# Two recurrence units abreast in the second half, and the whole short convolution beside the first recurrence

## The chip, the cores and the metric

The kernel runs on one core of one Trainium2 chip. The metric is the device time of one execution in microseconds (us). Three runs of the kernel before took 3340.84, 3342.81 and 3344.05 us, so the median is 3342.81 us.

## The reference, cut to what matters

The reference is one inference step of a two-layer trunk for a prompt of 1024 tokens and a group of 8 x 8 sample tokens that share all weights. All is float32. Only layer 0 is touched here:

```python
def mix_even(h, sc_buf, shift_prev, wkv0, p):
    z = h @ p['w_in']
    ya, sc_new = short_conv_mixer(z[..., :3 * SC_DIM], sc_buf, p['sc_conv_w'])     # B * conv3(C * h)
    yb, shift_new, wkv_new = rwkv7_mixer(z[..., 3 * SC_DIM:], shift_prev, wkv0, p)
    out = jnp.concatenate([ya, yb], axis=-1) @ p['w_out']
...
    # inside rwkv7_mixer, per head, with a 64 x 64 state S
    def step(S, inp):
        r_t, w_t, k_t, v_t, kk_t, a_t = inp
        S = (S * w_t[:, :, None, :]
             - jnp.einsum('bhij,bhj->bhi', S, kk_t)[..., None] * (kk_t * a_t)[:, :, None, :]
             + v_t[..., None] * k_t[:, :, None, :])
        return S, jnp.einsum('bhij,bhj->bhi', S, r_t)
```

After `mix_even` come a residual sum, an RMS norm (`nf0`), a SwiGLU feed-forward block with 22 x 128 hidden columns, another residual sum, and the norm of layer 1 (`nm1`).

## The kernel before

**Halves and dense tiles.** The tokens are cut into two halves. H0 has 576 columns (64 sample tokens and 512 of the prompt), H1 has the other 512 of the prompt. Each dense product is made in tiles of 128 output rows (`gemm_tile`, L209). Each float32 operand is split into a high and a low part, and each of the 8 steps of the inner dimension takes three matmuls (L204, L205, L206). A tile of H0 is 48 matmuls, 24 of 320 columns and 24 of 256; a tile of H1 is 24 matmuls of 512 columns. The activation of a half is held in 8 high and 8 low tiles, `hh0`/`hl0` for H0 and `hh1`/`hl1` for H1 (L186).

**The recurrence.** It is done in chunks of 64 tokens with many small matmuls. A `Unit` (L502) is one pair of heads for 256 tokens, so a half has 8 units, and H0 has a ninth one for the samples. A unit has three parts, all generators that yield after each dependent step: `prepare` (L521, 6 yields), `core` (L590, 28 yields for a prompt unit, 22 for the sample unit) and `finish` (L800, 4 yields). `recurrence` (L424) puts units into rounds: two to a round in H0 (`two`), one in H1. In a round all its cores step in turn, and beside them, one yield at a time, the `finish` of the round before and the `prepare` of the next (`together`, L446). A round of prompt units has 29 steps. The cores of a round depend on nothing of each other, but within one core each step waits for the one before: TensorE, then VectorE or ScalarE, then TensorE again. The second unit of a round (`alt`) takes its large tiles from tags of the feed-forward block (`x`, `hidh`, `hidl`), and a second pair of zero-padded operands `kr2`.

**How dense and small work are mixed.** `weave` (L485) takes one yield of dense work (mostly one dense tile) and then `rate` steps of the recurrence. This is the program's order. The tile framework makes each engine's order of it, earlier work of the program first, and fills with later work that it takes to be ready, so in the trace small matmuls stand in the middle of dense tiles.

**The order of layer 0** (L1537 to L1556). First the projection of H0. Then the first half of the mixing: `first()` (12 tiles of H0's short convolution, 14 of H1's projection, the first 3 tiles of H1's short convolution, `conv1`) with the recurrence of H0 at 5.5 steps per yield. H0's recurrence has 151 steps: 7 of the first `prepare`, 4 x 29, 23 of the sample unit, 5 of the last `finish`. Then the second half: `second()`, which is `ffn0(H0)`, with the recurrence of H1 at 6 steps per yield. `ffn0(H0)` has 86 yields: 2 while the mixing's result is loaded and split, 8 output-projection tiles, 10 of the norm `nf0`, 66 of the feed-forward block (6 to a group of two hidden tiles). 6 more tiles of `conv1` are put beside the first 6 yields of that norm (`beside`, L473; `fill`, L866). H1's recurrence has 244 steps, 7 + 8 x 29 + 5, so at 6 it is through after 41 of the 86 yields. Last come the norm `nm1` of H0 with the last 3 tiles of `conv1` beside it (L1554), and layer 1's dense products for H0.

**A norm** (`rms`, L227, and `rms_split`, L261) squares 8 tiles on ScalarE (L237), adds them on VectorE (L239), sums over the partitions with small matmuls (L245), takes the power on GpSimd (L224), spreads it with matmuls (L255), and then scales and splits each tile (L269, L218, L219). No dense tile of that half can start before the first of the 8 is split.

Of the kernel before, what the change touches and what calls it, by code (L numbers as in the profile page):

```python
# [19 lines left out]
P = 128  # L20
D = 1024
KT = 8
# [12 lines left out]
CDEC = math.exp(-0.5)  # L35
NEG = -1e30

RATE = (5.5, 6, 1.8, 1.8, 1)

QY = 2  # L40
VY = 3

CF = (3, 6)


class Half:
# [234 lines left out]
class Even:  # L281
# [118 lines left out]
    def project(self, H, h):  # L400
# [4 lines left out]
        for i in (12, 4, 0, 8, 5, 1, 9, 13, 6, 2, 10, 7, 3, 11):  # L405
# [15 lines left out]
                nc.sync.dma_start(k.zd[H.i][min(i, 12)], z)  # L421
            yield

    def recurrence(self, H):  # L424

        two = not H.i
        if two:
            kr = [self.k.bp.tile([P, 4, 128], F32, name="kr2", tag="x", bufs=8) for _ in range(2)]
            for h in range(2):
                self.k.nc.gpsimd.memset(kr[h][64 * (1 - h):64 * (2 - h)], 0.0)  # L430
            self.kr2 = kr
        us = [Unit(self, H, p, c0, two and p % 2) for c0 in (0, 256) for p in range(4)]
        if two:
            us.append(Unit(self, H, None, 0, 0))
        w = 2 if two else 1
        rounds = [us[i:i + w] for i in range(0, len(us), w)]
        yield from together([u.prepare() for u in rounds[0]])
        for i, r in enumerate(rounds):
            side = [u.finish() for u in rounds[i - 1]] if i else []
            if i + 1 < len(rounds):  # L440
                side += [u.prepare() for u in rounds[i + 1]]
            yield from together([u.core() for u in r], side)
        yield from together([u.finish() for u in rounds[-1]])
# [20 lines left out]
def drain(gen):  # L464

    while True:
        try:
            next(gen)
        except StopIteration as e:
            return e.value  # L470
# [31 lines left out]
class Unit:  # L502
# [9 lines left out]
    def et(self, name, bufs=2):  # L512
        return self.m.tile([P, 256], name, bufs)

    def ct(self, shape, name, bufs, tag):

        if self.alt:
            return self.m.k.bp.tile(shape, F32, name=name, tag=tag, bufs=8 if tag == "x" else GH + 1)
        return self.m.tile(shape, name, bufs)

    def prepare(self):  # L521
        m, cols, n = self.m, self.cols, self.n
# [67 lines left out]
    def core(self):  # L590

        m, cols = self.m, self.cols
        k = m.k
        nc = k.nc
        V, G, S = nc.vector, nc.gpsimd, nc.scalar
        mm = nc.tensor.matmul

        def c3(t):
            return t.rearrange("p (c s) -> p c s", s=64)

        def c4(t):
            return t.rearrange("p (c s) -> p c s", s=128)

        kr = m.kr2 if self.alt else m.krz
        kb = self.ct([P, 4, 128], "kb", 1, "x")
        for h, eng in enumerate((V, G)):
            hs = slice(64 * h, 64 * h + 64)
            for o, t in ((h, self.nb), (1 - h, self.k2)):
                eng.tensor_mul(kb[hs, :, 64 * o:64 * o + 64], c3(t)[hs], c3(self.eN)[hs])
        for h in range(2):  # L610
            hs = slice(64 * h, 64 * h + 64)
            for sl, i in cols:
                cs = slice(sl.start // 64, sl.stop // 64)
                V.scalar_tensor_tensor(kr[h][hs, cs, 0:64], c3(self.xk)[hs, cs], k.col("kk", i, hs), c3(self.eE)[hs, cs], op0=ALU.mult, op1=ALU.mult)
            G.tensor_mul(kr[h][hs, :, 64:128], c3(self.xr)[hs], c3(self.eP)[hs])
        yield
        mask = k.con("masks" if self.smp else "maskp")[:, None, :].to_broadcast([P, 4, 128])
        big = []
        for h in range(2):
            pb = k.bank()  # L620
            for c in range(4):
                mm(pb[:, 128 * c:128 * c + 128], kb[:, c], kr[h][:, c], start=True, stop=True)
            big.append(self.ct([P, 4, 128], "big", 2, "x"))
            V.tensor_mul(big[h], c4(pb), mask)
            yield

        def b4(name):
            return k.con(name)[:, None, :].to_broadcast([P, 4, 32])

        def tt(name, bufs=1):  # L630
            return self.ct([P, 4, 32], name, bufs, "hidh" if name == "tt" else "hidl")

        def c32(t):
            return t[:, 0:128].rearrange("p (c s) -> p c s", s=32)

        def each(o, lhs, rhs):
            for c in range(4):
                for q in Q:
                    mm(o[q, 32 * c:32 * c + 32], lhs[q, c], rhs[q, c], start=True, stop=True)

        HS = (slice(0, 64), slice(64, 128))
        Q = [slice(32 * i, 32 * i + 32) for i in range(4)]
        nt = self.ct([P, 4, 32], "nt", 1, "hidl")
        for i, q in enumerate(Q):
            (V.tensor_copy if i // 2 else S.copy)(nt[q], big[i // 2][q, :, 32 * (i % 2):32 * (i % 2) + 32])
        T1 = tt("tt", 2)
        V.tensor_mul(T1, nt, b4("m1t"))
        V.tensor_add(T1, T1, b4("i32"))
        full = self.ct([P, 4, 64], "full", 1, "x")
        G.memset(full, 0.0)  # L650
        st = self.ct([P, 4, 128], "st", 1, "x")
        vu = self.ct([P, 4, 128], "vu", 1, "x")
        yield
        for j, lv in enumerate((2, 4) if self.smp else (2, 4, 8, 16)):
            T0 = tt("t0")
            V.transpose(T0, T1)
            pw = k.bank()
            each(pw, nt, T0)
            W = tt("wm")
            V.tensor_mul(W, c32(pw), b4("m%d" % lv))  # L660
            yield
            pu = k.bank()
            each(pu, W, T1)
            T2 = tt("tt", 2)
            V.tensor_add(T2, T1, c32(pu))
            T1 = T2
            yield
            if j == 0:
                pt = k.bank()
                for c in range(4):  # L670
                    nc.tensor.transpose(pt[:, 128 * c:128 * c + 128], kb[:, c], k.con("ident"))
                S.copy(st, c4(pt))
                yield
            elif j == 1:
                pt = k.bank()
                for c in range(2):
                    nc.tensor.transpose(pt[:, 128 * c:128 * c + 128], self.xv[:, 128 * c:128 * c + 128], k.con("ident"))
                p4 = c4(pt[:, 0:256])
                for h, hs in enumerate(HS):
                    G.memset(vu[hs, :, hs], 0.0)  # L680
                    for e in range(2):
                        S.copy(vu[HS[1 - h], e::2, hs], p4[HS[e], :, hs])
                yield
        for i, q in enumerate(Q):
            S.copy(full[q, :, 32 * (i % 2):32 * (i % 2) + 32], T1[q])
        if not self.smp:
            T0 = tt("t0")
            V.transpose(T0, T1)
            W = tt("wm")
            pw = k.bank()  # L690
            for c in range(4):
                for h in range(2):
                    mm(pw[Q[2 * h + 1], 32 * c:32 * c + 32], big[h][Q[2 * h], c, 32:64], T0[Q[2 * h], c], start=True, stop=True)
            for h in range(2):
                V.tensor_copy(W[Q[2 * h + 1]], c32(pw)[Q[2 * h + 1]])
            yield
            pu = k.bank()
            for c in range(4):
                for h in range(2):
                    mm(pu[Q[2 * h], 32 * c:32 * c + 32], W[Q[2 * h + 1], c], T1[Q[2 * h + 1], c], start=True, stop=True)  # L700
            for h in range(2):
                V.tensor_copy(full[Q[2 * h], :, 32:64], c32(pu)[Q[2 * h]])
            yield
        T1 = full
        self.oo = self.et("oo", 3)
        yield from (self.samples if self.smp else self.chunks)(kr, big, st, vu, T1)
# [134 lines left out]

def out_ffn(k, H, l, fill=iter(()), last=None):


    nc, A = k.nc, k.A
    y = k.parts(H)
# [8 lines left out]
    for n in range(KT):  # L857
# [5 lines left out]
            nc.vector.tensor_add(x[:, a:b], x[:, a:b], gemm_tile(k, w, y, a, b))  # L863
        xs.append(x)
        yield
    h = yield from beside(rms_split(k, H, xs, "nf%d" % l), fill)  # L866
    for g in range(NF // GH):
        hid = []
        for f in range(GH * g, GH * g + GH):
# [619 lines left out]
def hybrid_step(tc, A, O):  # L1489
# [4 lines left out]
    with ExitStack() as es:  # L1494
# [15 lines left out]
        nc.sync.dma_start(k.pp, A["pp"])  # L1510
        k.load_con(cp, 0)

        def ffn0(H, fill=iter(())):
            xs = yield from out_ffn(k, H, 0, fill)
            for i in range(KT):
                nc.sync.dma_start(k.xs[H.i][i], xs[i])
            return xs
# [12 lines left out]
        with tc.tile_pool(name="m0", bufs=1) as mp, tc.tile_pool(name="mps", bufs=1, space=PSUM) as k.mps:  # L1530
# [6 lines left out]
            def first():  # L1537
                yield from m.short_conv(H0, h0)
                yield from m.project(H1, h1)
                yield from islice(conv1, CF[0])  # L1540

            def norm1():
                h1.extend((yield from rms_split(k, H1, x_in(H1), "nm0")))

            weave(m.project(H0, h0), norm1(), 1)
            x0 = []
            conv1 = m.short_conv(H1, h1)

            def second():
                x0.extend((yield from ffn0(H0, islice(conv1, CF[1]))))  # L1550

            weave(first(), m.recurrence(H0), RATE[0])
            weave(second(), m.recurrence(H1), RATE[1])
            h0 = drain(beside(rms_split(k, H0, x0, "nm1"), conv1))  # L1554
            drain(conv1)
            m.finish()  # L1556
        with tc.tile_pool(name="m1", bufs=1) as mp, tc.tile_pool(name="mps1", bufs=1, space=PSUM) as k.mps:
            m = Odd(k, mp)
# [146 lines left out]
```

## Time and profile before

| what | value |
|---|---|
| median of 3 runs | 3342.81 us |
| the profiled execution's own time | 3342.04 us |
| its span in the trace | 3340.3 us |
| TensorE (PE) busy with matmuls | 3169.4 us, 95% |
| PE weight loads (PEld) | 2666.9 us, 80% |
| VectorE (DVE) | 1906.4 us, 57% |
| ScalarE (ACT) | 1058.7 us, 32% |
| GpSimd (POOL) | 834.7 us, 25% |

Times in the trace count from the span's start. Matmuls are pipelined, and a matmul's modelled duration overlaps that of the next, so the distance from one start to the next is the time that a matmul costs in a full stream. "Idle" is time in which the engine ran nothing; an arrow shows what ended it.

### The profile page before, as it was taken

How to read it: one execution, taken by the hardware profiler on the slowest of the kernel's cores; microseconds unless marked ns; L12 is line 12 of the kernel's file. 1: busy time of each engine (PE TensorE's matmuls, PEld its weight loads, DVE VectorE, ACT ScalarE, POOL GpSimd, SP SyncE). 2: the span in 40 equal slices, each digit the busy share in tenths (PEclk: the TensorE clock that was granted, in tenths of full speed). 3: DMA queues.
4: the chain of work that ended last, by engine and by line, in shares of the span. 5: the costliest groups of instructions: out<-in, count | busy, mean ns of one | idle time of the engine just before them, and what ended most of it. 6: DMA issues, size and time to landing. Idle time of an engine off the chain costs nothing. (4 is left out here: it accounts for less than half of the span.)

```text
span 3340.3 us, 63263 instructions
## 1 busy us (share of the span) xinstructions
PE 3169.4 (95%) x25213; PEld 2666.9 (80%) x25213; DVE 1906.4 (57%) x3643; ACT 1058.7 (32%) x2083; POOL 834.7 (25%) x561
## 2 busy tenths in 40 slices
PE   7999999999999998999999998989999998999998
PEld 7887667777889997977677675766777776899998
DVE  6766646565544447556655457565545656554445
ACT  4333323332222223345322223332224553322222
POOL 4423333332333333301300103002010001333332
PEclk9999999999999998999999999999999999999999
DMA  5322333211122234544345656775554334232222
GB/s 178 116 59 79 87 96 118 73 59 56 51 66 83 83 108 148 191 151 135 108 135 163 199 154 213 240 221 175 172 171 138 113 110 135 87 105 81 83 83 78
DMA packets 238471, 409.20 MB, mean 123 GB/s; under 512 B 37632, under 2 KB 129664, under 8 KB 238176
## 3 DMA queue, kind: packets, MB, share of 16 engines
q10 hardware_dynamic: 63232, 218.80, 20.2%
q1 hardware_dynamic: 165584, 152.27, 15.4%
q0 software_dynamic: 9360, 34.08, 3.0%
q8 instruction: 199, 3.26, 0.4%
q14 instruction: 96, 0.79, 0.1%
HBM read 352.23 MB, written 52.81 MB: 121 GB/s over the span
## 5 line engine op out<-in xcount | busy, mean ns | idle before, releaser
L204 PE MATMUL acc<-hh,wh 128*128 128x320 f32 (+2 forms) x3720 | 1264.9, 341 | 17.6 <-ACT hh L218 14.7
L206 PE MATMUL acc<-hh,wl 128*128 128x320 f32 (+2 forms) x3720 | 1255.4, 338 | 7.4 <-POOL wl L198 6.5
L205 PE MATMUL acc<-hl,wh 128*128 128x320 f32 (+2 forms) x3720 | 1254.8, 338 | 7.2 <-DVE hl L219 5.4
L204 PEld LDWEIGHTS acc<-hh,wh 128*128 128x128 f32 x3720 | 712.3, 192 | 97.5 <-ACT hh L218 19.4
L198 POOL TENSOR_TENSOR wl<-wraw,wh 128x1024 fp32r<-128x1024 f32 x225 | 539.6, 2398 | 1000.6 <-ACT wh L196 924.7
L196 ACT CAST wh<-wraw 128x1024 fp32r<-128x1024 f32 (+1 forms) x398 | 416.0, 1045 | 1139.4 <-PE acc L205 1054.1
L206 PEld LDWEIGHTS acc<-hh,wl 128*128 128x128 f32 x3720 | 712.8, 192 | 74.7 <-issue 11.1
L205 PEld LDWEIGHTS acc<-hl,wh 128*128 128x128 f32 x3720 | 713.0, 192 | 72.1 <-DVE hl L219 9.1
L205 PE MATMUL acc<-hidl,wh 128*128 128x320 f32 (+2 forms) x1056 | 353.1, 335 | 0.6 <-DVE hidl L219 0.6
L893 DVE TENSOR_TENSOR x<-x,acc 128x320 f32<-128x320 f32 (+2 forms) x528 | 270.3, 527 | 139.1 <-PE acc L206 136.1
L206 PE MATMUL acc<-hidh,wl 128*128 128x320 f32 (+2 forms) x1056 | 349.5, 332 | 0.0
L204 PE MATMUL acc<-hidh,wh 128*128 128x320 f32 (+2 forms) x1056 | 348.9, 337 | 0.4 <-ACT hidh L218 0.4
L198 DVE TENSOR_TENSOR wl<-wraw,wh 128x1024 fp32r<-128x1024 f32 x173 | 210.9, 1219 | 145.3 <-ACT wh L196 143.2
L1297 POOL DMA_INDIRECT kv<-in_cv,vidx x64 | 75.5, 1180 | 628.8 <-DVE kt L1249 134.4
L204 PEld LDWEIGHTS acc<-hidh,wh 128*128 128x128 f32 x1056 | 198.7, 189 | 24.0 <-issue 4.2
L205 PEld LDWEIGHTS acc<-hidl,wh 128*128 128x128 f32 x1056 | 199.2, 189 | 19.1 <-issue 2.2
L206 PEld LDWEIGHTS acc<-hidh,wl 128*128 128x128 f32 x1056 | 199.5, 189 | 15.6 <-issue 1.4
L219 DVE TENSOR_TENSOR hidl<-ft,hidh 128x512 fp32r<-128x512 f32 (+2 forms) x148 | 178.7, 1207 | 55.9 <-ACT hidh L218 55.8
L881 DVE SCALAR_TENSOR_TENSOR ft<-ft,acc 128x320 f32<-128x320 f32 (+2 forms) x132 | 70.1, 531 | 213.1 <-PE acc L206 212.9
L875 DVE SCALAR_TENSOR_TENSOR ft<-ft,acc 128x320 f32<-128x320 f32 (+2 forms) x132 | 69.7, 528 | 177.0 <-ACT ft L874 176.8
L218 ACT CAST hidh<-ft 128x512 fp32r<-128x512 f32 (+2 forms) x148 | 75.1, 507 | 117.5 <-DVE ft L881 114.3
L1249 DVE STREAM_TRANSPOSE kt<-kv 128x1024 f32<-128x1024 f32 x64 | 79.3, 1239 | 33.8 <-DMA kv<-in_ck 29.9
(339 smaller groups left out, 3334.7 us busy)
## 6 DMA issues: line engine op xcount, KB each, us to landing
wraw<-in_wi ACTq DMA_DIRECT2D x100, 512.0 KB
wraw<-in_wg ACTq DMA_DIRECT2D x88, 512.0 KB
wraw<-in_wu ACTq DMA_DIRECT2D x88, 512.0 KB
wraw<-in_wd ACTq DMA_DIRECT2D x88, 512.0 KB
kv<-in_ck SPq DMA_DIRECT2D x512, 64.0 KB
wraw<-in_wo ACTq DMA_DIRECT2D x32, 512.0 KB
ka<-kp SPq DMA_DIRECT2D x48, 128.0 KB
x<-in_xT SPq DMA_DIRECT2D x16, 288.0 KB
```

What stands on the lines that cost most here:

```text
L196: nc.scalar.copy(wh, raw)
L198: k.low.tensor_sub(wl, raw, wh)
L204: mm(acc, wh, xh, start=first, stop=False)
L205: mm(acc, wh, xl, start=False, stop=False)
L206: mm(acc, wl, xh, start=False, stop=last)
L218: k.nc.scalar.copy(hh, v)
L219: (eng or k.nc.vector).tensor_sub(hl, v, hh)
L875: nc.vector.scalar_tensor_tensor(s[:, a:b], s[:, a:b], 1.0, pc, op0=ALU.add, op1=ALU.mult)
L881: nc.vector.scalar_tensor_tensor(s[:, a:b], s[:, a:b], 0.5, pu, op0=ALU.mult, op1=ALU.mult)
L893: nc.vector.tensor_add(xs[n][:, a:b], xs[n][:, a:b], acc[:, :b - a])
L1249: V.transpose(kt, kr)
L1297: nc.gpsimd.indirect_dma_start(out=v, out_offset=None, in_=A["cv"].rearrange("o (s r) c -> (o s) (r c)", r=2), in_offset=bass.IndirectOffs ...
```

## The change

H1's recurrence takes the two-abreast form of H0's. The second unit's tiles and H1's `kr2` lie in `hh1` and `hl1` (`self.lent`, `borrow`), H1's own activation, whose last reader is now the last tile of H1's short convolution. All 12 tiles of that convolution stand in `first()`, so the two norms of H0 have no dense tile of it beside them. The rates become 4.2 for the first half (38 yields, 159 steps due, 151 needed) and 2 for the second (H1's recurrence has 7 + 4 x 29 + 5 = 128 steps, through after 64 of 86 yields).

```diff
-RATE = (5.5, 6, 1.8, 1.8, 1)
+RATE = (4.2, 2, 1.8, 1.8, 1)
...
-CF = (3, 6)
...
+    def borrow(self, shape, name, i):
+        tag, bufs = self.lent[i]
+        return self.k.bp.tile(shape, F32, name=name, tag=tag, bufs=bufs)
+
     def recurrence(self, H):
...
-        two = not H.i
-        if two:
-            kr = [self.k.bp.tile([P, 4, 128], F32, name="kr2", tag="x", bufs=8) for _ in range(2)]
-            for h in range(2):
-                self.k.nc.gpsimd.memset(kr[h][64 * (1 - h):64 * (2 - h)], 0.0)
-            self.kr2 = kr
-        us = [Unit(self, H, p, c0, two and p % 2) for c0 in (0, 256) for p in range(4)]
-        if two:
+        self.lent = (("x", 8), ("hidh", GH + 1), ("hidl", GH + 1)) if not H.i else (("hh1", KT), ("hl1", KT), ("hl1", KT))
+        self.kr2 = [self.borrow([P, 4, 128], "kr2", 0) for _ in range(2)]
+        for h in range(2):
+            self.k.nc.gpsimd.memset(self.kr2[h][64 * (1 - h):64 * (2 - h)], 0.0)
+        us = [Unit(self, H, p, c0, p % 2) for c0 in (0, 256) for p in range(4)]
+        if not H.i:
             us.append(Unit(self, H, None, 0, 0))
-        w = 2 if two else 1
-        rounds = [us[i:i + w] for i in range(0, len(us), w)]
+        rounds = [us[i:i + 2] for i in range(0, len(us), 2)]
...
-    h = yield from beside(rms_split(k, H, xs, "nf%d" % l), fill)
+    h = yield from rms_split(k, H, xs, "nf%d" % l)
...
                 yield from m.project(H1, h1)
-                yield from islice(conv1, CF[0])
+                yield from m.short_conv(H1, h1)
...
-            conv1 = m.short_conv(H1, h1)
-
-            def second():
-                x0.extend((yield from ffn0(H0, islice(conv1, CF[1]))))
-
             weave(first(), m.recurrence(H0), RATE[0])
-            weave(second(), m.recurrence(H1), RATE[1])
-            h0 = drain(beside(rms_split(k, H0, x0, "nm1"), conv1))
-            drain(conv1)
+            weave(keep(ffn0(H0), x0), m.recurrence(H1), RATE[1])
+            h0 = drain(rms_split(k, H0, x0, "nm1"))
```

The other lines of the diff pass the index of the lent tag through `Unit.ct`.

## Rows read from the trace of the kernel before

**Rows 1.** The page's head and its line of engines: busy us (share of the span) and instructions of each.

```profile
span 3340.3 us, 63263 instructions
PE 3169.4 (95%) x25213; PEld 2666.9 (80%) x25213; DVE 1906.4 (57%) x3643; ACT 1058.7 (32%) x2083; POOL 834.7 (25%) x561
```

**Rows 2.** Windows over three stretches of layer 0: the first half of the mixing, the second half until H1's recurrence is through, and the rest of the feed-forward block. Columns: stretch, its length, then busy us (instructions) of each engine, PEclk (the granted share of TensorE's clock), the DMA share and GB/s.

```profile
128.40:516.50 388.10, 365.37 (x4768) 280.69 (x4766) 237.64 (x623) 121.36 (x325) 126.19 (x110) 0.96 0.29 86
516.50:974.00 457.50, 427.55 (x5122) 356.83 (x5123) 267.27 (x642) 136.00 (x332) 138.15 (x104) 0.97 0.21 66
974.00:1231.00 257.00, 257.00 (x1921) 256.20 (x1920) 104.83 (x179) 62.28 (x96) 96.24 (x40) 1.00 0.25 83
```

**Rows 3.** Timeline rows of ACT and DVE that read the result of a dense tile (start us, duration us, engine, line, operation): the last of H0's projection, the last of `conv1` in the first half, the same step of two groups of the feed-forward block that are six tiles apart, and two neighbouring tiles of `conv1`.

```profile
128.42 0.47 ACT L395 ACTIVATE ft<-acc,dv 128x256 f32<-128x256 f32 x1
...
516.52 0.68 DVE L369 TENSOR_TENSOR ft<-ft,acc 128x512 f32<-128x512 f32 x1
...
1029.59 0.49 DVE L875 SCALAR_TENSOR_TENSOR ft<-ft,acc 128x320 f32<-128x320 f32 x1 [0.60 <-ACT ft L874]
...
1068.17 0.49 DVE L875 SCALAR_TENSOR_TENSOR ft<-ft,acc 128x320 f32<-128x320 f32 x1 [0.60 <-ACT ft L874]
...
1256.04 0.68 DVE L354 TENSOR_TENSOR up<-ft,acc 128x512 f32<-128x512 f32 x1
...
1261.69 0.68 DVE L369 TENSOR_TENSOR ft<-ft,acc 128x512 f32<-128x512 f32 x1
```

**Rows 4.** Timeline rows of PE that begin a round's first large product (L622): the first and the second round of the first half, the first (533) and the last (894) of the second half's eight.

```profile
153.35 0.39 PE L622 MATMUL rk<-krz,kb 128*128 128x128 f32 x1
...
225.01 0.27 PE L622 MATMUL rk<-krz,kb 128*128 128x128 f32 x1
...
533.17 0.63 PE L622 MATMUL rk<-krz,kb 128*128 128x128 f32 x2
...
894.42 0.38 PE L622 MATMUL rk<-krz,kb 128*128 128x128 f32 x2
```

**Rows 5.** Windows of line L206 alone (one of the three matmuls of each dense step): stretch, length, PE busy (matmuls), PEld busy (loads), clock, DMA. The first two stretches are rounds of the first half, the first with tiles of H0, the second with tiles of H1. The next five are rounds of the second half with tiles of H0 alone. The last is a stretch without recurrence.

```profile
153.30:225.00 71.70, 25.69 (x79) 15.63 (x79) 0.93 0.20 56
299.20:368.30 69.10, 17.71 (x41) 7.67 (x40) 0.98 0.30 85
533.20:581.10 47.90, 19.40 (x62) 11.68 (x62) 0.97 0.22 74
692.00:738.50 46.50, 15.42 (x47) 9.37 (x47) 0.92 0.16 46
738.50:781.90 43.40, 16.36 (x51) 9.59 (x51) 1.00 0.21 70
781.90:838.60 56.70, 23.11 (x70) 14.69 (x70) 0.91 0.17 53
838.60:894.40 55.80, 24.24 (x80) 15.15 (x80) 1.00 0.17 54
1000.00:1050.00 50.00, 36.65 (x124) 23.36 (x124) 1.00 0.24 79
```

**Rows 6.** Timeline of PE in the first half's second round, some 4 us of it: dense matmuls, then bursts of two units' small ones.

```profile
238.97 0.31 PE L205 MATMUL acc<-hl,wh 128*128 128x320 f32 x1
239.11 0.31 PE L206 MATMUL acc<-hh,wl 128*128 128x320 f32 x1
239.35 0.45 PE L639 MATMUL rk<-t,nt 32*32 32x32 f32 x32
...
241.05 0.75 PE L639 MATMUL rk<-tt,wm 32*32 32x32 f32 x64
241.73 0.38 PE L206 MATMUL acc<-hh,wl 128*128 128x256 f32 x1
```

**Rows 7.** Waits of PE over three rounds of the first half (153.3 to 368.3): who waited for whom, us in total, times, the longest. The first and the last of nine rows, which add up to 9.1 us.

```profile
PE rk L639 <- DVE wm L660: 3.3, 2, 1.9
...
PE rk L828 <- DVE tt L665: 0.3, 1, 0.3
```

**Rows 8.** The norm `nm1`: windows over the end of the last three tiles of `conv1`, the stretch with no dense matmul, and the three after it (columns as in group 2); then the norm's own two groups of matmuls in PE's timeline.

```profile
1243.00:1260.50 17.50, 17.50 (x81) 14.18 (x79) 8.87 (x12) 6.89 (x10) 6.32 (x3) 1.00 0.46 166
1260.50:1269.30 8.80, 4.00 (x22) 3.44 (x21) 5.45 (x15) 1.92 (x3) 5.51 (x6) 0.64 0.72 235
1269.30:1276.00 6.70, 6.34 (x31) 4.72 (x31) 6.70 (x16) 3.73 (x6) 3.98 (x3) 0.71 0.12 48
1276.00:1282.50 6.50, 4.69 (x31) 4.06 (x31) 6.46 (x8) 2.03 (x3) 3.55 (x3) 1.00 0.01 3
1282.50:1289.00 6.50, 4.98 (x39) 4.98 (x40) 6.30 (x7) 2.05 (x4) 1.44 (x1) 1.00 0.43 106
...
1261.76 1.28 PE L245 MATMUL acc<-con,ft 128*128 128x1 f32 x10 [1.08 <-DVE ft L239]
1265.48 2.50 PE L255 MATMUL acc<-con,rs 128*128 128x64 f32 x10 [2.44 <-POOL rs L224]
```

**Rows 9.** The norm `nf0`: the window of the six tiles of `conv1` beside it (columns as in group 2), and the one long wait of PE in the feed-forward block's first tile.

```profile
617.30:681.30 64.00, 60.64 (x644) 42.58 (x644) 40.04 (x94) 23.58 (x54) 22.51 (x16) 1.00 0.22 69
...
687.61 0.41 PE L205 MATMUL acc<-hl,wh 128*128 128x320 f32 x1 [2.77 <-DVE hl L219]
```

**Rows 10.** GpSimd's clearing of H0's second operand pair (`kr2`, whose tile is named kr): count, shortest, median and longest duration in ns, first and last start. And the longest wait of PE between 500 and 550 us, where the halves meet.

```profile
L430 POOL MEMSET kr<- x2: 521/522/522, 78.0 to 80.5; 64x512 f32 x2
...
PE acc L204 <- ACT hh L218: 1.8, 1, 1.8
```

More of the change, by code (lines that the diff above doesn't have):

```diff
@@ L513, in et, with ct @@
         return self.m.tile([P, 256], name, bufs)
[L515 to L519, printed above, removed]
+    def ct(self, shape, name, bufs, lent):
+        return self.m.borrow(shape, name, lent) if self.alt else self.m.tile(shape, name, bufs)
     def prepare(self):
@@ L604, in core @@
         kr = m.kr2 if self.alt else m.krz
-        kb = self.ct([P, 4, 128], "kb", 1, "x")
+        kb = self.ct([P, 4, 128], "kb", 1, 0)
         for h, eng in enumerate((V, G)):
@@ L622, in core @@
                 mm(pb[:, 128 * c:128 * c + 128], kb[:, c], kr[h][:, c], start=True, stop=True)
-            big.append(self.ct([P, 4, 128], "big", 2, "x"))
+            big.append(self.ct([P, 4, 128], "big", 2, 0))
             V.tensor_mul(big[h], c4(pb), mask)
@@ L630, in tt @@
         def tt(name, bufs=1):
-            return self.ct([P, 4, 32], name, bufs, "hidh" if name == "tt" else "hidl")
+            return self.ct([P, 4, 32], name, bufs, 1 if name == "tt" else 2)
         def c32(t):
@@ L642, in core @@
         Q = [slice(32 * i, 32 * i + 32) for i in range(4)]
-        nt = self.ct([P, 4, 32], "nt", 1, "hidl")
+        nt = self.ct([P, 4, 32], "nt", 1, 2)
         for i, q in enumerate(Q):
@@ L648, in core @@
         V.tensor_add(T1, T1, b4("i32"))
-        full = self.ct([P, 4, 64], "full", 1, "x")
+        full = self.ct([P, 4, 64], "full", 1, 0)
         G.memset(full, 0.0)
-        st = self.ct([P, 4, 128], "st", 1, "x")
-        vu = self.ct([P, 4, 128], "vu", 1, "x")
+        st = self.ct([P, 4, 128], "st", 1, 0)
+        vu = self.ct([P, 4, 128], "vu", 1, 0)
         yield
@@ L840, in finish, with out_ffn @@
             nc.sync.dma_start(k.ysp0[self.H.i][4 + i][:, self.ts], oo[:, sl])
-def out_ffn(k, H, l, fill=iter(()), last=None):
+def out_ffn(k, H, l, last=None):
     nc, A = k.nc, k.A
@@ L1511, in hybrid_step, with ffn0 @@
         k.load_con(cp, 0)
-        def ffn0(H, fill=iter(())):
-            xs = yield from out_ffn(k, H, 0, fill)
+        def ffn0(H):
+            xs = yield from out_ffn(k, H, 0)
             for i in range(KT):
```

## The prediction, made before the run

> **What bounds the kernel now.** The first thing to read is the page's head and its line of engines [rows 1]: TensorE is busy 95% of the span and no other engine over 57%, so a gain must come out of TensorE's own time. The second is the same split by stage [rows 2]. In the rest of the feed-forward block, where nothing but dense tiles runs, weight loads fill 256.2 of 257.0 us. In the first half they fill 280.7 of 388.1 (72%), in the second 356.8 of 457.5 (78%). So the two mixing stages hold time that dense work doesn't use. The third thing is the pace of dense tiles [rows 3]: six tiles of H0 take 1068.17 - 1029.59 = 38.58 us, 6.43 each, and a tile of H1 takes 1261.69 - 1256.04 = 5.65.
>
> From these I get what each half costs beyond its dense tiles. The first half runs from 128.42 to 516.52 [rows 3], 388.1 us. It holds 12 tiles at 6.43 and 17 at 5.65, 173.2 us, which leaves 215 for nine units. The second runs to about 974 [rows 2], 457.5 us. It holds 32 tiles at 6.43 (8 of the output projection, four groups of the feed-forward block) and 6 at 5.65, 239.7 us, which leaves 218 for eight units. Fewer units, more time: that is what the change can win.
>
> **The change part by part.**
>
> *Pairs in place of single units.* I price a round, from one round's first large product to the next's [rows 4]: its length less its dense steps. 124 dense steps take 50 us where nothing else runs, 0.403 us each [rows 5]; a step of H1 takes 5.65/8 = 0.706. The first half's round from 153.3 is 71.7 us with 79 steps: 71.7 - 31.9 = 39.8 us for two units. The one from 299.2 is 69.1 - 41 x 0.706 = 40.2. The five rounds of the second half that have tiles of H0 alone leave 22.9, 27.5, 22.8, 28.5 and 23.5, on average 25.0 us for one unit, 50.1 for two. A pair saves 50.1 - 40.0 = 10.1 us, four pairs 40. The work itself is the same; what shrinks is the number of times that TensorE turns from dense to small work and back, and the waits at those turns. The timeline shows it [rows 6]: two dense matmuls start 0.14 us apart, 0.24 us pass from the last of them to a small one, and a burst of 64 small matmuls from both units takes 0.68 us and is followed by one such turn, not two.
>
> *Two steps to a tile in place of 5.5.* No row shows a pair at this rate. PE's waits over three rounds of the first half are 9.1 us, 3 a round [rows 7], most of them for VectorE's half of a step. At two steps per tile some 3.2 us of dense work (6.43/2) fall to each step, against about 1.1 in the first half (31.9 us over 29 steps), so I take half of the waits away: 4 x 1.5 = 6 us. Bounds: nothing, and all of it with some turns, 24 us (6 a round). In the first half, 4.2 steps per tile against 5.5 is a small move; I cost it at nothing, within 8 us either way. If H0's recurrence were late at the end of its half, the cover would be gone and its rest would run bare, but 151 steps are due after 36 of 38 yields.
>
> *The norm `nf0` loses its six tiles.* Those six tiles take 33.9 us of the 64.0 beside which the norm ran [rows 9], and all that was left of it for TensorE was a wait of 2.8 us for the split. They now stand in the first half, at the same 5.65 each, so their own time moves and doesn't change. Nearest row of a bare norm: `nm1` [rows 8]. From 1260.5 to 1289.0, 28.5 us, there are 123 matmuls, of which 101 are dense and 22 are the norm's or last ones before it. 101 at 0.134 (0.403/3) are 13.5, so a bare norm loses 15.0 us, in part at half clock (the granted clock is 0.64 in the 8.8 us with next to no matmul and 0.71 in the 6.7 us behind them, mixes of its two levels of 1.2 and 2.4 GHz). In `nf0` the recurrence of H1 still runs, 20 steps of pairs by the program's order, but VectorE has both. I take half of the bare norm, 7 us. Bounds: 0 and 15.
>
> Against the change stands a rule of the Trainium skill ("TensorE: Matmul & The Clock Gate", section "Why this matters for your kernels"): keep TensorE fed between bursts, or its clock falls back. The trace agrees at `nm1`, where it fell to the lower level in the norm [rows 8]; at `nf0` it was at 1.00 with the tiles beside it [rows 9]. By the rule `nf0` costs nearer 15 than 7, and the sum would be 8 us later.
>
> *The norm `nm1` loses its three tiles.* The 17.5 us of tiles ended before the bare stretch began [rows 8]: VectorE's last additions came only then, and the power and the matmuls after it stood alone. So these tiles hid little. They go to the first half at their price; the bare stretch grows by the last tile's addition, square and sum. I take 2 us; bounds -3 (additions no longer behind the convolution's on VectorE) and 6.
>
> *What costs nothing, and why.* Each of `conv1`'s tiles brings its weight DMA and cast on ACT's queue, its low part on POOL and its output on SP's queue wherever it stands, as the 17 H1 tiles of the first half do now. The new `kr2` costs GpSimd two clearings of 0.52 us [rows 10], which wait for the last `conv1` tile's reads of `hh1`. Behind them on GpSimd stand the low parts of weights, for which the output projection would wait; but that tile's reads of a high part end with TensorE still in it, and the weights are made about two tiles ahead. If that cover is gone it costs one low part, some us, once. The meeting of the halves, where PE waits 1.8 us for the first split [rows 10], keeps its shape. What is late next, once the pairs run, is the small matmuls' own time and the dense tiles: TensorE stays the bound.
>
> **Sum.** The profiled execution took 3342.0 us: a span of 3340.3 and 1.7 around it; the median of the runs is 0.8 above. Pairs -40, waits at the lower rate -6, `nf0` +7, `nm1` +2: -37 us, which from either figure gives **3305 us**. All bounds at their low ends at once give 3267 (-40, -24, -8, 0, -3), at their high ends 3331 (-40, 0, +8, +15, +6); the forecast's own range is 3289 to 3315.
>
> **The rivals.**
>
> *Turns cost less than I think (faster still).* At two steps to a tile each step finds its inputs done, both units' bursts and the side's stand in one block, and a round falls from the 38.5 that I forecast (40.0 - 1.5) to about 34. That is 18 us in the second half, and 8 in the first, whose rate falls too: 3279. For it: the waits of [rows 7]. Against it: the turns of [rows 6] stay, at least one a step.
>
> *The norms eat half.* `nf0` 15, `nm1` 6, no waits saved: -40 + 21 = -19, 3323. For it: [rows 8]. Against it: H1's recurrence has ready work throughout `nf0`. The clock rule named above points here.
>
> *The pair falls apart (slower).* With more dense work ready between the steps, each unit's burst is set down by itself, with a turn on both sides. Then a pair costs what two single units cost, 50.1, and the saving is nil, while the norms are bare all the same: +15 and +2, 3359. It decides from the point at which a round costs over 50.1 - 9/4 = 47.9 us. For it: the first half has 31.9 dense us in a round, the second would have 29/2 x 6.43 = 93, so dense matmuls lie ready far more often, and already in the first half bursts of x32 of one unit stand alone [rows 6]. Against it: bursts of x64 are there too, though 5.5 steps to a tile leave each step less time for both units to be ready.
>
> *It isn't abreast.* If the second unit's tiles in `hh1` came free late, the two cores would run one behind the other: the price of single units with `nf0` at 7 and `nm1` at 2, 3351. Against it: eight slots serve as many tiles in the first half's `x`.
>
> A rule of the skill tells two ways of reading apart ("Perfetto Trace Analysis", section "Identifying the Most-Contended Engine"): matmul busy time is a poor measure of headroom, weight-load time a better one. By matmul busy time both halves are alike (365.4 of 388.1 and 427.6 of 457.5 [rows 2]); it would leave pairs nothing to gain and the sum at +9, 3351. The rounds' price [rows 5] speaks for the page.
>
> **How the numbers follow.** Forecast (3289 to 3315) 0.57; faster still (3270 to 3289) 0.16; norms eat half (3315 to 3333) 0.14; falls apart 0.09; not abreast 0.04. The bound for no change is 0.2%, 6.7 us, about what a measurement of this kernel can tell. The first three lie below 3336: faster 0.86, with 0.01 of them lost to the edge. Not abreast and the mild end of falling apart: same 0.04 (pairs at 46.2 to 49.5 us, which with +9 is within 6.7 of no change), slower 0.10. For 8 in 10 the range holds the forecast, about 0.10 of the faster case and 0.13 of the norms' case: 3281 to 3330.
>
> **What would show it.** Right: rounds of H1 with two units (L622 bursts on both operand pairs) at 37 to 41 us beyond their dense steps; the first half some 49 us longer (nine tiles at 5.65, 50.9); the feed-forward block free of small matmuls after some 64 yields; a stretch of PE at lower clock at `nf0` worth about 7 us; `nm1` as before without the three tiles. Wrong: a round above 47.9 us, `nf0` above 15, or the first half longer by over 60.

## The result, and the profile after

The changed kernel takes 3362.38 us (median of 4 runs, 3356.4 to 3364.2) against 3342.57 for the kernel before: a ratio of 1.0056, 95% interval 1.0039 to 1.0074. The forecast was 3305 us. The time went up by 20 us where it should have gone down by 37. The profiled execution took 3361.41 us, with a span of 3359.6.

The page's head and line of engines, which answer to [rows 1], show next to nothing: TensorE is busy 4 us less in a span 19 us longer.

```profile
span 3359.6 us, 63232 instructions
PE 3165.5 (94%) x25213; PEld 2680.5 (80%) x25213; DVE 1922.2 (57%) x3643; ACT 1056.7 (31%) x2083; POOL 833.8 (25%) x563
```

The line of the whole span with TensorE's mean granted clock shows more. Before:

```profile
core 0: 3340.3 us, clock 0.974
```

After:

```profile
core 0: 3359.6 us, clock 0.964
```

I call (1 - clock) x length the lost clock: 86.8 us before (0.026 x 3340.3), 120.9 after (0.036 x 3359.6). It rose by 34 us, more than the span did. Span times clock fell from 3253 to 3239. By this measure the change took some 15 us of work out of the kernel, and the clock took 34 back.

Where? Windows by stage of the kernel before (columns as in group 2 of the rows above): output projection of H0, the norm `nf0` up to the first result of the feed-forward block, that block up to its last group, `nm1` with the first tiles behind it, and the rest. The first half is in [rows 2].

```profile
516.50:617.30 100.80, 92.92 (x1162) 79.32 (x1163) 59.51 (x144) 29.37 (x70) 30.16 (x22) 0.97 0.29 92
617.30:705.10 87.80, 81.53 (x873) 60.12 (x874) 59.98 (x135) 33.12 (x76) 33.18 (x27) 0.98 0.21 66
705.10:1209.80 504.70, 488.90 (x4850) 452.38 (x4849) 245.96 (x533) 130.31 (x273) 163.81 (x92) 0.98 0.21 68
1209.80:1302.70 92.90, 84.41 (x552) 78.15 (x551) 63.24 (x93) 31.71 (x48) 38.17 (x22) 0.94 0.40 125
1302.70:3340.30 2037.60, 1952.96 (x12300) 1615.26 (x12299) 1153.80 (x1927) 653.80 (x1187) 385.05 (x241) 0.98 0.46 144
```

The same stages of the changed kernel, the first half ahead of them:

```profile
129.70:578.10 448.40, 418.14 (x4998) 323.10 (x4997) 257.05 (x651) 132.91 (x337) 147.96 (x121) 0.96 0.29 89
578.10:658.10 80.00, 72.80 (x786) 66.97 (x790) 62.81 (x114) 28.47 (x60) 30.55 (x23) 0.96 0.30 99
658.10:712.90 54.80, 51.47 (x568) 39.69 (x564) 31.65 (x88) 19.49 (x54) 13.30 (x14) 0.63 0.08 25
712.90:1234.60 521.70, 492.12 (x5382) 463.80 (x5383) 275.06 (x601) 134.76 (x299) 170.35 (x102) 0.97 0.22 71
1234.60:1312.80 78.20, 68.65 (x479) 66.52 (x478) 52.04 (x76) 26.77 (x42) 28.38 (x15) 0.89 0.38 115
1312.80:3359.60 2046.80, 1959.01 (x12301) 1620.16 (x12299) 1157.11 (x1927) 655.36 (x1188) 385.08 (x241) 0.97 0.45 143
```

With the moved tiles taken out at 5.65 us each (9 into the first half, 6 out of `nf0`, 3 out of `nm1`), the first half is 9.4 us longer (448.4 - 388.1 - 50.9), the output projection 20.8 shorter, `nf0` 0.9 longer (54.8 - 53.9), the feed-forward block 17.0 longer, `nm1` 2.3 longer, the rest 9.2 longer. Summed over windows of 2 us, 19 of the 34 us of lost clock came up in `nf0` and 10 in the rest, behind `nm1`. The row to look at is `nf0`: a granted clock of 0.63, so 20.3 of its 54.8 us are lost clock, against 1.8 before. In windows of 25 us:

```profile
650.00:675.00 25.00, 21.52 (x427) 18.14 (x426) 13.26 (x36) 8.40 (x25) 5.89 (x3) 0.79 0.17 55
675.00:700.00 25.00, 25.00 (x170) 17.85 (x171) 10.89 (x33) 7.23 (x22) 4.53 (x4) 0.50 0.01 1
700.00:725.00 25.00, 22.46 (x273) 19.65 (x272) 17.62 (x48) 11.56 (x29) 10.07 (x12) 0.89 0.18 54
```

The reader should see a TensorE that is, by the profile, busy for all 25.00 us at half clock. VectorE is busy 10.89 of 25, so it isn't the limit there. The whole stretch at the lower level (1.2 GHz) is 41 us long:

```profile
664.40:705.40 41.00, 39.74 (x363) 29.65 (x363) 20.00 (x60) 13.22 (x40) 9.46 (x12) 0.50 0.04 11
```

PE's timeline in that stretch shows what runs: small matmuls of the pairs' chunks, and from 674.8 between them the first feed-forward tile, one to four matmuls at a time:

```profile
680.14 0.85 PE L202 MATMUL acc<-hh,wh 128*128 128x320 f32 x2
680.92 0.48 PE L742 MATMUL ch<-ys,full 64*64 64x64 f32 x4
681.33 0.48 PE L730 MATMUL ch<-vu,st 128*64 128x64 f32 x4
681.74 0.64 PE L203 MATMUL acc<-hl,wh 128*128 128x320 f32 x1
682.18 0.47 PE L204 MATMUL acc<-hh,wl 128*128 128x320 f32 x1
682.45 0.41 PE L203 MATMUL acc<-hl,wh 128*128 128x256 f32 x1
...
683.64 0.64 PE L202 MATMUL acc<-hh,wh 128*128 128x320 f32 x1
684.20 0.48 PE L730 MATMUL ch<-vu,st 128*64 128x64 f32 x4
```

Two dense matmuls that follow each other there start 0.27 us apart (682.18 and 682.45), against 0.14 at full clock [rows 6].

The pairs' rounds, priced as in [rows 5], from three windows of L204 (the third matmul of a dense step, L206 before) between starts of rounds:

```profile
611.30:703.30 92.00, 29.41 (x93) 19.16 (x93) 0.79 0.14 46
703.30:833.00 129.70, 64.45 (x212) 41.15 (x212) 0.97 0.22 70
833.00:967.00 134.00, 67.56 (x225) 42.86 (x224) 0.99 0.20 65
```

The first round, which holds `nf0`, costs 92.0 - 93 x 0.403 = 54.5 us, of which 19 are lost clock (0.21 x 92.0). The next two cost 129.7 - 212 x 0.403 = 44.2 us and 134.0 - 225 x 0.403 = 43.3: under the 47.9 from which pairs would lose, over the 38.5 of the forecast.

### The profile page after: what moved, and what is told of

It reads as the page before. It is cut to its first block, busy times and chain, and to the rows that moved or that the text cites. A ratio compares the mean times of both kernels' runs of the same rounds, so it can differ in the third digit from the quotient of the medians.

```text
span 3359.6 us, 63232 instructions
## 1 busy us (share of the span) xinstructions
PE 3165.5 (94%) x25213; PEld 2680.5 (80%) x25213; DVE 1922.2 (57%) x3643; ACT 1056.7 (31%) x2083; POOL 833.8 (25%) x563
## 5 line engine op out<-in xcount | busy, mean ns | idle before, releaser
L204 PE MATMUL acc<-hh,wl 128*128 128x320 f32 (+2 forms) x3720 | 1253.7, 337 | 7.9 <-POOL wl L196 7.8
L204 PEld LDWEIGHTS acc<-hh,wl 128*128 128x128 f32 x3720 | 715.7, 192 | 71.4 <-POOL wl L196 10.7
L204 PE MATMUL acc<-hidh,wl 128*128 128x320 f32 (+2 forms) x1056 | 351.6, 334 | 0.0
L204 PEld LDWEIGHTS acc<-hidh,wl 128*128 128x128 f32 x1056 | 202.2, 191 | 15.8 <-issue 1.4
L871 ACT ACTIVATE ft<-acc 128x320 f32<-128x320 f32 (+2 forms) x132 | 61.8, 469 | 117.9 <-PE acc L204 115.1
```

The costliest lines, as they stand in the source:

```text
L204: mm(acc, wl, xh, start=False, stop=last)
L871: nc.scalar.activation(s[:, a:b], pc, AF.Tanh, scale=0.5)
```

## The experiments

Two theories stood after the result. **A:** the loss is in the bare norm `nf0`, where small matmuls at half clock stand ahead of the first dense tile. **B:** pairs spread at two steps to a tile cost 45 us a round wherever the norm stands. No kernel leaves work out; e6 adds some.

| kernel | median us | ratio to before (95%) | span | clock | span x clock |
|---|---|---|---|---|---|
| before | 3342.6 | 1 | 3340.3 | 0.974 | 3253 |
| changed | 3362.4 | 1.0056 (1.0039, 1.0074) | 3359.6 | 0.964 | 3239 |
| e1 norm in one | 3327.4 | 0.9959 (0.9947, 0.9971) | 3321.5 | 0.976 | 3242 |
| e2 rate 5.5 | 3357.1 | 1.0036 (1.0022, 1.0050) | 3360.0 | 0.964 | 3239 |
| e3 late pairs | 3331.1 | 0.9969 (0.9957, 0.9981) | 3321.2 | 0.975 | 3238 |
| e4 late single | 3361.9 | 1.0061 (1.0048, 1.0073) | 3360.1 | 0.976 | 3279 |
| e5 single | 3380.3 | 1.0121 (1.0105, 1.0137) | 3379.8 | 0.967 | 3268 |
| e6 spare tiles | 3382.7 | 1.0121 (1.0104, 1.0139) | 3382.7 | 0.967 | 3271 |
| e7 norm, first rate | 3321.1 | 0.9948 (0.9934, 0.9961) | 3313.7 | 0.975 | 3231 |
| e8 norm, rate 5.5 | 3345.6 | 1.0017 (1.0003, 1.0031) | 3336.4 | 0.970 | 3236 |
| e9 rates | 3317.3 | 0.9937 (0.9919, 0.9955) | 3311.9 | 0.974 | 3226 |

Spans and clocks are of the one profiled execution, which lies up to 8 us from its kernel's median.

**e1: no steps inside the norm.**

```diff
-    h = yield from rms_split(k, H, xs, "nf%d" % l)
+    h = drain(rms_split(k, H, xs, "nf0")) if H is H0 else (yield from rms_split(k, H, xs, "nf%d" % l))
```

> The changed kernel, but the norm nf0 of H0 is one yield of the dense work: no step of H1's recurrence is due inside it, so the first feed-forward tile stands ahead of the steps that came before it. Theory A (in the bare norm TensorE runs small matmuls of the pairs at half clock, 41 us without a break, and the first dense tile waits behind them): the half-clock stretch at nf0 shrinks to 10 to 17 us and the kernel takes 3345 to 3353 us. Theory B (pairs at two steps per tile cost 45 us a round and not 40, wherever the norm stands): 3358 to 3365 us, rounds beyond the first still at 45.

3327.4 us, 35.0 below the changed kernel and 15 below the kernel before. Theory A, and by more than it said: the lower level lasts 3.4 us at `nf0` (662.4 to 665.8), not 10 to 17. Its windows of `nf0` and the feed-forward block:

```profile
657.00:679.00 22.00, 17.80 (x319) 15.63 (x312) 16.36 (x39) 9.34 (x18) 9.22 (x6) 0.92 0.08 25
679.00:1200.30 521.30, 500.60 (x5631) 469.38 (x5631) 283.79 (x648) 143.83 (x335) 174.12 (x110) 0.99 0.23 72
```

`nf0` falls from 54.8 to 22.0 us. The steps that no longer run there must run later, yet the feed-forward block isn't longer (521.3 against 521.7). The clock accounts for most of it: lost clock falls in `nf0` from 20.3 to 1.8 and in the block from 15.7 (0.03 x 521.7) to 5.2, together 29 of the 33 us. (Summed over windows of 2 us the block goes from 13.7 to 3.4, and the two together come to the same 29.) Its rounds, in L204's windows:

```profile
609.60:742.00 132.40, 66.83 (x226) 42.67 (x225) 0.99 0.20 65
742.00:880.00 138.00, 72.00 (x241) 45.45 (x241) 1.00 0.23 73
880.00:1011.00 131.00, 67.92 (x225) 43.01 (x224) 0.99 0.22 66
```

41.3, 40.9 and 40.3 us (132.4 - 226 x 0.403 and so on): the first half's price of 40.0, at two steps to a tile. Theory B falls with its second half too: spread steps cost no more.

The norm of e1 isn't empty: its window has 319 matmuls, most of them small ones of the pairs that were ready. But from 667.8 the first feed-forward tile runs in one piece there.

**e2: 5.5 steps to a tile in the second half.** `RATE = (4.2, 5.5, ...)` in the changed kernel.

> The changed kernel with 5.5 steps per dense yield in the second half in place of 2. Theory B (sparse steps cost more): the three rounds after the norm fall from 45 to 40 us beyond their dense steps, the kernel to 3344 to 3350 us. Theory A (the norm at half clock): 55 steps are due inside the norm, so the half-clock stretch is as long or longer than 41 us and the kernel takes 3360 to 3375 us.

3357.1 us (3346.3 to 3361.8), 5 below the changed kernel, 3 under A's range and 7 over B's. The time alone doesn't decide. The norm's window, from the output projection's end to the first result of the feed-forward block, is now longer, at 0.71:

```profile
702.20:790.70 88.50, 78.03 (x1180) 60.56 (x1181) 57.11 (x172) 29.68 (x91) 20.89 (x24) 0.71 0.11 31
```

0.29 x 88.5 = 25.7 us of lost clock, more than the changed kernel's 20.3, as A has it; but it comes in four stretches at the lower level, the longest of 23.5 us, and not in one of 41 or more. The two rounds that hold the norm cost 55 us each, so B's fall to 40 didn't come.

**e3 and e4: cover for the norm, with pairs and with single units.** Both put six tiles of H1's convolution back beside `nf0` and begin H1's recurrence behind it, 20 yields late; e4 has one unit to a round. The rates are 4.8 and 2.2 in e3, 4.8 and 3.8 in e4. The edit of e3:

```diff
-                yield from m.short_conv(H1, h1)
+                yield from islice(conv1, 6)
...
-    h = yield from rms_split(k, H, xs, "nf%d" % l)
+    h = yield from beside(rms_split(k, H, xs, "nf%d" % l), fill)
...
-            weave(keep(ffn0(H0), x0), m.recurrence(H1), RATE[1])
+            weave(keep(ffn0(H0, conv1), x0), chain(repeat(None, 44), m.recurrence(H1)), RATE[1])
```

> Pairs in the second half as in the changed kernel, but six tiles of H1's short convolution stand beside nf0 again, and H1's recurrence begins only after that norm, at 2.2 steps per yield of the feed-forward block (first half at 4.8, with six tiles of that convolution). Theory A: nf0 runs at full clock, the 19 us of clock lost there come back and the output projection runs without turns: 3325 to 3343 us, rounds at 40 to 45. Theory B: rounds stay at 45 to 47 and the kernel at 3350 to 3360 us.

> The same as e3_late_pairs with one unit to a round, at 3.8 steps per yield: the only difference is single units against pairs. If a pair saves the 10 us of the forecast, this is 40 us above e3_late_pairs; if only 5 a pair (50 against 45), 20 us above; if spread steps take the saving away altogether, within 7 us of it.

e3 took 3331.1 us, in A's range. e4 took 3361.9, 30.8 above it. The two differ in nothing else but the rate that single units need, so this is what pairs are worth here: 7.7 us a pair by the medians, against 10.1 in the forecast. The rate isn't what differs through the clock: span times clock is 3231 to 3238 us over e3's twelve executions and 3267 to 3279 over e4's five. The profiled executions lie 38.9 us apart (3360.1 - 3321.2), but at the first matmul of `nm1`, ahead of which all pairs are done, they are only 26.4 apart, 6.6 a pair. First e3, then e4:

```profile
1247.82 1.01 PE L243 MATMUL acc<-con,ft 128*128 128x1 f32 x4 [6.39 <-DVE ft L237]
...
1274.23 0.59 PE L243 MATMUL acc<-con,ft 128*128 128x1 f32 x2 [5.76 <-DVE ft L237]
```

By rounds the forecast's price comes out. Three rounds of e3 and seven of e4, in L204's windows:

```profile
679.20:1050.30 371.10, 188.90 (x625) 119.49 (x624) 0.99 0.21 68
...
662.60:1180.00 517.40, 258.17 (x852) 162.32 (x851) 0.99 0.21 65
```

(371.1 - 625 x 0.403)/3 = 39.7 us for a pair, just under A's 40 to 45, and (517.4 - 852 x 0.403)/7 = 24.9 for one unit, 49.7 for two. That is 10.0 us a pair; why the times show only 6.6 to 7.7 of it, no run separates.

**e5: single units in the changed kernel.** As e4's edit, in the changed kernel, 4 steps per yield.

> The changed kernel with one unit to a round in the second half, at 4 steps per yield: the convolution moved and the norms bare, but no pairs. If pairs save what e3 against e4 showed (31 us) wherever they stand, 3385 to 3400 us. If the bare norm's loss is one of pairs alone (two units' small matmuls in the way), the half-clock stretch at nf0 is under 17 us and the time at most 3370.

3380.3 us, between the two. Pairs save 17.9 us in this layout, not 31. With single units `nf0` loses less clock, in two stretches of 10 us at the lower level. So the stretch is under 17 us, as it should be if the loss were one of pairs alone, but the time isn't at most 3370:

```profile
666.20:709.00 42.80, 37.56 (x480) 28.91 (x479) 28.74 (x76) 14.63 (x36) 12.24 (x9) 0.76 0.10 29
```

0.24 x 42.8 = 10.3 us against 20.3. So a bare norm filled with small work loses clock with either, and twice as much with pairs.

**e6: useless dense tiles beside the norm.**

```diff
+def spare(k):
+    for i in range(6):
+        w = load_w(k, k.A["wi0"][i])
+        acc = k.bank("acc")
+        for j in range(KT):
+            mm3(k, acc, w[0][:, 0:128], w[1][:, 0:128], w[0][:, 512:1024], w[1][:, 512:1024], j == 0, j == KT - 1)
...
-    h = yield from rms_split(k, H, xs, "nf%d" % l)
+    norm = rms_split(k, H, xs, "nf%d" % l)
+    h = yield from (beside(norm, spare(k)) if H is H0 else norm)
```

> The changed kernel with six spare dense tiles beside nf0 (24 matmuls of 512 columns each, made of a weight with itself, their results read by nobody): 33.9 us of work that the kernel doesn't need, at the place where the convolution's tiles stood. Clock theory (the loss at nf0 is half clock under small matmuls alone): the stretch of half clock shrinks from 41 us to 10 or less, and the kernel is only 5 to 20 us above the changed one, 3367 to 3382, far less than the 33.9 us that it adds. Order theory (the loss is that the first feed-forward tile stands behind the steps, whatever the clock): the kernel is 30 to 40 us above, 3392 to 3402.

3382.7 us: 33.9 us of work nobody needs cost 20.3, 0.7 over the top of the clock theory's range and far from the order theory's. The stretch at the lower level is 13.8 us, where 10 or less was expected. The window of `nf0`:

```profile
657.00:732.60 75.60, 72.33 (x709) 57.30 (x710) 36.39 (x90) 30.14 (x69) 28.05 (x20) 0.91 0.19 58
```

It is 20.8 us longer than the changed kernel's 54.8, and its lost clock is 6.8 (0.09 x 75.6) in place of 20.3: 33.9 - 13.5 = 20.4. The clock alone makes up the difference in this window.

**e7, e8, e9: the rates, with the norm in one.** `RATE` of (5.5, 2), (4.2, 5.5) and (5.5, 1.75) in e1.

> e1_norm_in_one with 5.5 steps per yield in the first half in place of 4.2. If the first half's 8 us beyond its dense tiles are due to the lower rate, 3317 to 3322 us and a first half near 439 us; if they are due to the nine tiles themselves beside the sample unit, no change, 3324 to 3331.

> e1_norm_in_one with 5.5 steps per yield in the second half in place of 2, the norm still without steps. If the lower rate saves waits, as the forecast's term of 6 us has it, rounds rise from 41.5 to 43 us and the kernel to 3330 to 3336; if the rate doesn't matter once the norm is clear, 3322 to 3332 with rounds at 40 to 42.

> e7_norm_first_rate with 1.75 steps per yield in the second half in place of 2 (133 steps due over its 76 yields, 128 needed). If more dense work between the steps still raises the clock, 3313 to 3319 us; if 2 is low enough, 3317 to 3325; if the last steps and layer 1's early instructions now meet at the end of the feed-forward block, above 3325.

e7 took 3321.1 us, 6.3 below e1. The runs of the two overlap (3315.5 to 3326.5 against 3323.4 to 3333.3), but the first half decides: 436.5 us where e1's is 447.0. All eight profiles at 4.2 have it at 447 to 451 us, the two at 5.5 (e7, e9) at 437 and 438. So the lower rate, not the nine tiles, cost the first half its 8 to 9 us.

```profile
128.20:564.70 436.50, 413.73 (x4999) 319.91 (x4997) 255.94 (x652) 132.03 (x337) 148.90 (x121) 0.97 0.31 92
```

e8 took 3345.6 us (3335.9 to 3359.5), 18 above e1 and outside what either line expected. In its profile the clock is 0.970 against e1's 0.976 while span times clock is 6 us less; over all its executions the clock is 0.964 to 0.970, over e1's 0.970 to 0.976. Its round behind the norm costs 70.7 - 81 x 0.403 = 38.1 us, no more than e1's:

```profile
752.30:823.00 70.70, 25.49 (x81) 15.10 (x80) 1.00 0.18 57
```

So a lower rate in the second half does pay once no step falls due inside the norm, through the clock and not through fewer waits. In the changed kernel, where they do, e2's higher rate cost nothing. e9 took 3317.3 us (3313.7 to 3327.6), 3.8 below e7, a difference that these runs can't tell from none. It is the fastest version, 0.63% under the kernel before.

**The second profiles.**

> The changed kernel once more, for a second profile. Clock theory: the half-clock stretch at nf0 is there again, 30 us or longer, and nothing like it elsewhere in layer 0. If layer 1's 10 us of further clock loss belong to the change, they are there again (57 us lost behind nm1, give or take 4); if they are chance from execution to execution, the second profile differs by more.

> e1_norm_in_one once more, for a second profile. Clock theory: no stretch of half clock over 10 us at nf0, and 1.7 to 7 us lost there. Layer 1's loss as for after_again: near 48 us if it belongs to the kernel, else anywhere from 40 to 62.

One run each: 3364.47 us with a clock of 0.965, and 3319.48 with 0.975. The half-clock stretch at `nf0` of the changed kernel is there again, 41 us long, and e1 has none over 3.5 us again. The stretch of the one and the norm's window of the other:

```profile
665.50:706.50 41.00, 40.09 (x362) 29.34 (x361) 20.43 (x60) 12.60 (x39) 8.88 (x11) 0.50 0.05 15
...
658.30:680.30 22.00, 17.80 (x319) 15.68 (x316) 16.43 (x38) 9.30 (x18) 9.25 (x6) 0.92 0.08 25
```

Behind `nm1` the changed kernel loses 51 us of clock where its first profile had 57 (windows of 2 us). That is outside the 4 us allowed, so by the expectation's own rule the further loss of clock there is at least in part chance. The stage takes 2047 us in both profiles all the same, so lost clock doesn't turn into time there one for one. e1 takes 2043.5 us in one profile and 2037.9 in the other, the kernel before 2037.6. Whether the 9 us behind `nm1` belong to the change stays open.

## Why the prediction was wrong

**The step that failed** is the one on `nf0`: "I take half of the bare norm, 7 us. Bounds: 0 and 15." It holds a wrong picture of the cover. I read the recurrence's ready steps as work that fills the bare norm and so lessens the loss. They did fill it, and TensorE was busy for all of the 25 us from 675. But it ran them at half clock, and they stood in the program's order ahead of the first feed-forward tile, whose matmuls came one to four at a time between them. The upper bound, taken from `nm1` [rows 8], is of a norm that no step stands ahead of, which is cheaper: in e1, where none falls due inside it, `nf0` took 22.0 us from end to end. (Of the 15.0 us read from `nm1`, 2.3 are no loss of the norm's either: they are a wait of PE at 1284 us for a result of layer 1's scan.) What the step is worth is 35.0 us, changed kernel against e1, and e1 differs only in when H1's steps fall due. e6 shows the clock's part by itself: with dense tiles beside the same steps `nf0` lost 6.8 us of clock in place of 20.3. What raises the clock again these runs don't show: in e1 it rose at 665.8, ahead of the dense tile.

The rule of the Trainium skill that the prediction weighed ("TensorE: Matmul & The Clock Gate", section "Why this matters for your kernels") pointed to the right place; the price that I gave it, 15, was too low by more than half. The trace goes beyond it: the rule speaks of gaps between bursts, and here the clock stayed at the lower level while PE was busy 39.74 of 41.0 us.

**The miss by stages.** The profiled execution is 56 us above the forecast. The three stages of the second half are 36 of them (-3 in place of -39), the first half 9, and the stretch behind `nm1` 9, for which the sum had no term. All three signs of being wrong came: a round above 47.9 (the first, 54.5), `nf0` above 15, and the first half longer by over 60 (448.4 - 388.1 = 60.3).

**Pairs, -40.** Right in kind, and in the price of a round: 39.7 us in e3 and 40.3 to 41.3 in e1, against the forecast's 40.0. In time it is less, 30.8 us between the medians of e4 and e3 and 26.4 in layer 0 of their profiles.

**Waits at the lower rate, -6.** Wrong as told: e1's rounds are at 40.8 on average, not 38.5. A lower rate did gain, 18 us between e8 and e1, by the clock, but not while steps fell due inside the norm (e2).

**First half, 0 within 8.** It was 9.4 us longer, just outside. e7 shows the rate of 4.2 as its cause.

**`nm1`, +2.** 2.3 us. Right.

**Edits at nothing.** Right: between 560 and 615 us PE's waits are all for VectorE (4.3 us at L583, 2.8 at L826, 1.1 at the first split), none for the clearings or the weights behind them. But one move wasn't foreseen (below).

**The rivals.** "The pair falls apart" gave 3359 us, near the measured time, and is false: rounds clear of the norm are at 44 us, not 50, and pairs save time in both layouts tried (e3 against e4, the changed kernel against e5). "The norms eat half" named the right place with too small a price. That its time fits is luck; the rounds decide.

**The sum again.** The second half's three stages, without the moved tiles, went from 659.4 us (693.3 - 33.9) to 656.5 in the changed kernel and to 624.1 in e1. The forecast was -39; it is -35 once the norm is clear.

## What to carry to other kernels

A stage that keeps TensorE busy isn't yet a cover: small matmuls that fill the hole left by dense ones can leave the engine busy at half clock, and then the work in the hole and the dense work behind it pay double (0.27 us for 0.14 from one dense matmul to the next). So before taking dense tiles away from beside a norm, ask what will run in their place, and price the hole by (1 - granted clock) x length, not by idle time. When small work has slack, let none of it fall due inside a stretch without dense work: here one line that does so turned a loss of 20 us into a gain of 15.

## What the runs showed that I hadn't expected

Span times clock sorts these kernels better than their times do. Over all executions the versions with pairs and no spare work lie between 3220 and 3245 us, those with single units between 3249 and 3279, while the spans themselves overlap. The lost clock moves by up to 40 us between kernels whose work is the same (changed kernel 120.9, e1 79.7), and by 20 within one kernel (e1 80 to 100).

Instructions of layer 1 that prepare its attention moved. Before, VectorE ran their long scan behind `nm1`, at 1278 us; in the changed kernel it runs at 1134, inside the feed-forward block, some 24 us behind the end of H1's recurrence. VectorE waited there for a transfer, and TensorE for the split that stood behind it:

```profile
1133.31 1.17 DVE L1089 COPY pl<-plf 128x512 f32<-128x512 f32 x2 [3.56 <-DMA plf<-in_clf,pidx]
1134.52 4.32 DVE L1093 TENSOR_TENSOR_SCAN plf<-prs,pl 128x1024 f32<-128x1024 f32 x1
```

```profile
PE acc L203 <- DVE hidl L217: 5.6, 1, 5.6
```

In e1 the scan stands at 1172 us and no wait of PE from 1120 to 1210 us is over 2.4 us, so the wait of 5.6 us in the changed kernel can account for the 4 us of e1's gain that its clock leaves open. In all the variants the scan starts some 18 to 36 us behind the end of the recurrence. That fits a move because layer 0's last tiles now come free earlier, but this was not tried by itself.
